# Sorted sync queue, held side streams and the gating norm on ScalarE, in a two-layer hybrid decoder trunk

## Chip, cores, metric

One Trainium2 chip, all 8 cores, one batch element per core, no exchange between cores. The metric is the device time of the slowest core in microseconds (us), lower is better. Executions come in two states: *fast*, and *slow*, in which one die (cores 0 to 3 or 4 to 7) or both run at a lower granted TensorE clock. Only fast executions are compared; where a kernel had few of them, the text says so and uses the cores of an undisturbed die (their longest span). An execution that counts as fast can still hold a short stretch at the lower clock (0.81 in the clock records); where the clock records show one that matters, the text says it.

## The reference

Two layers, each a feed-forward, a mixer and a second feed-forward, every one behind an RMSNorm with a shift, scale and gate computed from a conditioning vector; sequence 4096, width 1024, hidden width 2816.

```python
for l in range(DEPTH):
    mod = c_act @ ada_w[l] + ada_b[l]                 # "ada" columns: shift, scale, gate x 3
    y = modulate(rmsnorm(h, norm_g[l, 0]), sh1, sc1)
    h = h + 0.5 * g1 * swiglu(y, ffn1_wg[l], ffn1_wu[l], ffn1_wd[l])
    y = modulate(rmsnorm(h, norm_g[l, 1]), sh2, sc2)
    u_a, v_a, q_b, k_b, v_b = split(y @ w_in[l])
    out_a = spatial_gating(u_a, v_a, ...)             # gelu, layer norm of v, 128x128 causal matmul
    out_b = dilated_mixture(rope(q_b), rope(k_b), v_b)   # 8 heads, three window/dilation patterns
    h = h + g2 * (concat([out_a, out_b]) @ w_out[l])
    y = modulate(rmsnorm(h, norm_g[l, 2]), sh3, sc3)
    h = h + 0.5 * g3 * swiglu(y, ffn2_wg[l], ffn2_wu[l], ffn2_wd[l])
return rmsnorm(h, final_g)
```

## The kernel before

Everything is unrolled at build time. `Sched` collects five instruction lists, one per engine, in *program order*, and adds semaphore waits from the buffers that an operation reads and writes. The TensorE's list is therefore a static order. The main stream (feed-forward, projections) calls `tick(ns)` after each piece, and `Mix` spends that credit on *side streams*: norms of the next tiles, attention, the conversion of float32 weights to bf16 copies in DRAM, the ada columns. h (`hS`), the normed input (`y2S`), q, k, v (`qS`, `kS`, `vS`) and the mixer's output (`mS`) travel through DRAM.

```python
def dma(self, eng, key, fn, reads=(), writes=(), accw=(), extra=()):
    ...
    self._waits(eng, self._deps(reads, writes, accw, extra))   # eng "sp": one queue, program order
    ...
class Mix:
    def tick(self, ns):
        for s in list(self.sides):
            s[1] += ns
            while s[1] > 0 and s in self.sides:
                ...
                s[1] -= next(s[0])          # emit one unit of the side stream, pay its cost

def conv_gen(l, w, cost): ...               # wguS/wdS <- wgu/wd, DRAM to DRAM, issued by POOL
def norm_load(t, src, bsrc):                # one 2 MB load
    Sx.dma("sp", "h", lambda e: e.dma_start(out=hbuf[0], in_=src[t]), ...)
def norm_steps(cost, mode, l, i, t, src, bsrc, y=0, gate=None, load=True, head=3):
    norm_load(t, src, bsrc)
    for _ in range(head):
        yield cost
    for q in range(4):
        norm_sq(2 * q); norm_sq(2 * q + 1)          # ScalarE squares (L535)
        if q: norm_mm(2 * q - 2); norm_mm(2 * q - 1)  # TensorE sums (L540)
        yield cost
    ...

def load_res(q):                            # feed-forward: residual tile of h for the down projection
    Sx.dma("sp", "hres%d" % (q % 3), lambda e: e.dma_start(out=ap, in_=src[tiles[s], :, m, :]), ...)
def down(q):                                # 22 matmuls (L668), then h + gate * result on VectorE (L675)
    ...
    Sx.dma("sp", "hres%d" % (q % 3), lambda e: e.dma_start(out=hS[t, :, m, :], in_=ap), ...)
    ...
def mixer_prep(l, t0, out):                 # 20 loads of w_in (512 KB float32 each) at once, issued by POOL
    for c in (1, 2, 0, 3, 4):
        for q in range(4):
            Sx.dma("pool", "win%d" % c, lambda e, n=n: e.dma_start(out=mx.win[0][:, n], in_=win_d[l, n]), ...)
        ...
def vnorm(s):                               # layer norm of the gating values, VectorE (L840)
    for hd in range(4):
        Sx.op("dve", lambda e, k_=k_, hd=hd: e.tensor_scalar(
            out=vh[:, hd, :], in0=vg[:, hd, :], scalar1=mv[:, k_, 0:1], scalar2=rs[:, k_:k_ + 1],
            op0=ALU.subtract, op1=ALU.mult), ...)
def load_qk(p):                             # attention, head pair p
    for h in range(2):
        srck = bass.AP(kS.tensor, kS.offset + row, [[128 * S, 2], [S, 32], [1, n]])
        ...                                 # and the same for q: four loads
def outproj(l, tiles, ox, banks, loaded, flag):
    ...
    for i, (t, m) in enumerate(pairs):
        ...                                 # 8 matmuls (L1158)
        ...                                 # h + gate * result on VectorE (L1163)
        Sx.dma("sp", "oh%d" % (i % 6), ... out=hS[t, :, m, :], in_=ap ...)
        load_h(i + 4)                       # residual tile of h, six buffers
```

The softmax here doesn't subtract the row's maximum and nothing guards it: scores larger than these inputs give would overflow.

Of the kernel before, what the change touches and what calls it, by code (L numbers as in the profile page):

```python
# [6 lines left out]
F32 = mybir.dt.float32  # L7
# [49 lines left out]
class Sched:  # L57
    ENG = ["pe", "act", "dve", "pool", "sp"]

    def __init__(self, nc, stack):  # L60
# [8 lines left out]
        self.sym = {e: [] for e in self.ENG}  # L69

# [44 lines left out]
    def op(self, eng, fn, reads=(), writes=(), accw=(), sig=True, extra=()):  # L115
        self._waits(eng, self._deps(reads, writes, accw, extra))
        if sig:
            self.cnt[eng] += 1
            s = self.sem[eng]
            self.q[eng].append(lambda e, fn=fn, s=s: fn(e).then_inc(s, 1))  # L120
            self.sym[eng].append(("i", ("e", eng), 1))
            tok = ("e", eng, self.cnt[eng])
        else:
            self.q[eng].append(fn)
            tok = ("e", eng, self.cnt[eng] + 1)
# [3 lines left out]
    def dma(self, eng, key, fn, reads=(), writes=(), accw=(), extra=()):  # L129
# [3 lines left out]
        self._waits(eng, self._deps(reads, writes, accw, extra))  # L133
        self.dcnt[key] += 16
        s = self.dsem[key]
        self.q[eng].append(lambda e, fn=fn, s=s: fn(e).then_inc(s, 16))
        self.sym[eng].append(("i", ("d", key), 16))
        tok = ("d", key, self.dcnt[key])
        self._mark(tok, reads, writes, accw)
        return tok  # L140

# [57 lines left out]
def build_nc():  # L199
# [37 lines left out]
    with ExitStack() as st:  # L237
# [62 lines left out]
        class Mix:  # L300
# [9 lines left out]
            def tick(self, ns):  # L310
                for s in list(self.sides):
                    s[1] += ns
                    while s[1] > 0 and s in self.sides:
# [5 lines left out]
            def until(self, s, cond):  # L319
                while not cond():  # L320
                    next(s[0])

            def drain(self, s):
                if s in self.sides:
                    for _ in s[0]:
                        pass
                    self.sides.remove(s)
# [73 lines left out]
        def ada_mm(ap, b, col):  # L401
            for kc in range(KC):
                Sx.op("pe", lambda e, kc=kc: e.matmul(ps[:, 7, col:col + 1], lhsT=ap[:, kc, :], rhs=cact[:, kc:kc + 1],
                                                      start=(kc == 0), stop=(kc == KC - 1)),
                      reads=[b, bConst], accw=[psB[7]], sig=(kc == KC - 1))
# [18 lines left out]
        def ada_gen(lo, cols, cost):  # L424
# [3 lines left out]
            def load(i):  # L428
                ap, b = ring[i % n]
                Sx.dma("pool", "adar%d" % (i % n), lambda e: e.dma_start(out=ap, in_=ada_w[cols[i]]), writes=[b])  # L430
# [3 lines left out]
            for i, col in enumerate(cols):  # L434
                if i + n - 1 < len(cols):
                    load(i + n - 1)
                ap, b = ring[i % n]
                ada_mm(ap, b, col)
# [8 lines left out]
        class Weights:  # L447
# [6 lines left out]
            def load_gu(self):  # L454
# [10 lines left out]
                if g == 0:  # L465
                    Sx.dma("pool", "gud%d" % s, lambda e: e.dma_start(out=ap, in_=wgu_d[l, w, j]), writes=[b])
# [5 lines left out]
            def load_wd(self):  # L472
# [10 lines left out]
                if g == 0:  # L483
                    Sx.dma("pool", "wdd%d" % s, lambda e: e.dma_start(out=ap, in_=wd_d[l, w, m]), writes=[b])
                else:
                    assert bWD[l, w, m].w, ("not converted", l, w, m)
                    Sx.dma("sp", "wd%d" % s, lambda e: e.dma_start(out=ap, in_=wdS[l, w, m]),
                           reads=[bWD[l, w, m]], writes=[b])
# [24 lines left out]
        def conv_gen(l, w, cost):  # L513
            toks = [None] * 4
            i = 0
            for j in range(FC):
                toks[i % 4] = Sx.dma("pool", "cv%d" % (i % 4), lambda e, j=j: e.dma_start(out=wguS[l, w, j], in_=wgu_d[l, w, j]),
                                     writes=[bWG[l, w, j]], extra=[toks[i % 4]])
                i += 1
                yield cost  # L520
            for m in range(KC):
                toks[i % 4] = Sx.dma("pool", "cv%d" % (i % 4), lambda e, m=m: e.dma_start(out=wdS[l, w, m], in_=wd_d[l, w, m]),
                                     writes=[bWD[l, w, m]], extra=[toks[i % 4]])
# [6 lines left out]
        def norm_load(t, src, bsrc):  # L530
            Sx.dma("sp", "h", lambda e: e.dma_start(out=hbuf[0], in_=src[t]), reads=bsrc[t], writes=hbuf[1])

        def norm_sq(kc):
            ap, b = sqr[kc % 4]
            Sx.op("act", lambda e: e.activation(out=ap, in_=hbuf[0][:, kc, :], func=AF.Square),  # L535
                  reads=[hbuf[1][kc]], writes=[b])
# [38 lines left out]
        def norm_steps(cost, mode, l, i, t, src, bsrc, y=0, gate=None, load=True, head=3):  # L575

            if load:
                norm_load(t, src, bsrc)
                for _ in range(head):
                    yield cost  # L580
            for q in range(4):
                norm_sq(2 * q)
# [9 lines left out]
            while gate is not None and not gate():  # L592
                yield cost
# [24 lines left out]
        def ffn_group(l, which, tiles, src, bsrc, posts=(), nxt=(), lag=0, hook=None):  # L618
# [35 lines left out]
            def load_res(q):  # L654
                if q < len(dn):
# [3 lines left out]
                           reads=[bsrc[tiles[s]][m]], writes=[b])  # L659

            def down(q):
# [5 lines left out]
                for j in range(FC):  # L667
# [4 lines left out]
                    if j in (7, 14):  # L672
# [6 lines left out]
                       reads=[b], writes=[bHS[t][m]])  # L679
                tick(7.4 * MM)  # L680

            sp_ = mix.add(seq(*[norm_steps(4000.0, *p) for p in posts])) if posts else None
            sn_ = None
            for j in range(FC + lag):
                for s in range(2):
                    jj = j - (lag if s else 0)
                    if 0 <= jj < FC:
                        gate(s, jj)
                        if s == 1:
                            if g == 0:  # L690
                                W.keep_gu(jj)
# [735 lines left out]
```

## Time and profile before

| | before |
|---|---|
| time, median | 6319.25 us over four executions (6304.29 to 6319.44 fast, one slow at 6548.12) |
| TensorE idle in the profiled execution | 1220.7 us of 6311.8 |
| TensorE busy at half clock | 442 us, so 221 us lost |
| TensorE waits for q/k loads | 306.7 us |
| TensorE waits for sums of squares | 335.0 us |

A waits line has the waiting engine and line, what ended the wait, and then us in total, number of waits, longest. First the TensorE's small waits for the two residual sums (L675 in the feed-forward, L1163 in the output projection):

```profile
PE ps L1158 <- DVE arena L1163: 20.4, 4, 6.6
...
PE ps L668 <- DVE arena L675: 3.9, 1, 3.9
```

Then what VectorE waits for in the same two lines:

```profile
DVE arena L675 <- DMA arena<-hS: 399.8, 52, 45.8
...
DVE arena L1163 <- DMA arena<-hS: 137.7, 45, 36.3
```

VectorE often waits for residual tiles, yet hardly anyone waits for VectorE: several PSUM banks lie between.

### The profile page before, as it was taken

Reading aid. Unit: us, or ns where it says so; the run is one execution under the profiler, and the core shown is the slowest. Engines: PE = TensorE matmul, PEld = TensorE weight load, DVE = VectorE, ACT = ScalarE, POOL = GpSimd, SP = SyncE. Lnnn points to the kernel's source line nnn. Section 1 sums busy time; section 2 is a strip of 40 time slices with the busy share of each in tenths; the row PEclk is TensorE's granted clock in tenths of the full one; section 3 lists DMA queues with packets and bytes.
Section 4 is the critical chain, followed back from the end, with each engine's and each line's share of the span. In section 5 each row is a group of like instructions: output and inputs, shape, how many; then the busy total and the mean of one; then the engine's idle time right before and its main releaser. Section 6 shows DMA issues by size and latency. Waiting matters only on the chain.

```text
span 6311.8 us, 82365 instructions; the slowest of 8 cores (6270.0 to 6311.8 us)
## 1 busy us (share of the span) xinstructions
PE 5091.1 (81%) x27299; PEld 2363.6 (37%) x27826; DVE 2475.9 (39%) x4066; ACT 1838.4 (29%) x2653; POOL 588.9 (9%) x631
## 2 busy tenths in 40 slices
PE   6887768887858787689997997888868677787997
PEld 2333324443323333334443443444323333343443
DVE  2232554342634333133332337544437333433442
ACT  2220323451313333122121214344322233422321
POOL 1001220001310000100001002100022000010000
PEclk9988889998879898789998998999989888988998
DMA  8878553535464553676478554344263634336444
GB/s 178 198 181 180 160 118 97 172 103 136 132 172 127 134 136 90 146 210 172 132 182 155 177 166 136 106 129 141 96 160 116 192 92 149 130 116 216 161 156 127
DMA packets 433581, 927.65 MB, mean 147 GB/s; under 512 B 157168, under 2 KB 206704, under 8 KB 419056
## 3 DMA queue, kind: packets, MB, share of 16 engines
q1 hardware_dynamic: 388912, 785.62, 39.1%
q0 software_dynamic: 44256, 136.73, 14.3%
q8 instruction: 234, 3.83, 0.3%
q14 instruction: 179, 1.47, 0.1%
HBM read 861.26 MB, written 249.56 MB: 176 GB/s over the span
## 4 chain that ended last, share of the span: by engine, by line
PE 55%; DMA 27%; DVE 4%; ACT 4%; issue 4%; POOL 3%; SPq 2%; another core or an unknown queue 1%; DVEq 0%; ACTq 0%; POOLq 0%
PE ps L637 32%; PE ps L668 11%; DMA arena<-hS 8%; DMA arena<-qS 8%; PE ps L806 5%; DMA hS<-arena 3%; DMA arena<-xP 3%; PE ps L1058 2%; POOL arena L1092 2%; PE ps L1029 2%; PE ps L540 2%; DMA vS<-arena 2%; DMA arena<-ada_w 1%; PE ps L1158 1%; DMA mS<-arena 1%
## 5 line engine op out<-in xcount | busy, mean ns | idle before, releaser
L637 PE MATMUL ps<-arena 128*128 128x512 bf16 x10961 | 2588.7, 387 | 100.5 <-DVE arena L645 35.3
L637 PEld LDWEIGHTS ps<-arena 128*128 128x128 bf16 x11264 | 1080.8, 99 | 1348.3 <-issue 177.8
L668 PE MATMUL ps<-arena 128*128 128x512 bf16 x5489 | 1296.5, 390 | 174.2 <-DMA arena<-wdS 154.2
L645 DVE SCALAR_TENSOR_TENSOR arena<-arena,ps 128x512 f32<-128x512 f32 x704 | 483.0, 686 | 1329.0 <-ACT arena L642 1307.7
L668 PEld LDWEIGHTS ps<-arena 128*128 128x128 bf16 x5632 | 548.6, 100 | 827.8 <-issue 239.6
L642 ACT ACTIVATE arena<-ps 128x512 f32<-128x512 f32 x704 | 419.3, 596 | 1355.4 <-PE ps L637 1170.6
L647 DVE TENSOR_TENSOR arena<-ps,arena 128x512 bf16<-128x512 f32 x704 | 486.9, 692 | 442.8 <-PE ps L637 405.3
L675 DVE SCALAR_TENSOR_TENSOR arena<-ps,arena 128x512 f32<-128x512 f32 x256 | 192.1, 750 | 1139.5 <-PE ps L668 431.8
L806 PE MATMUL ps<-arena 128*128 128x512 bf16 x2522 | 606.4, 397 | 6.2 <-DVE arena L675 1.9
L1036 ACT ACTIVATE arena<-ps 128x1024 bf16<-128x1024 f32 (+1 forms) x384 | 358.1, 933 | 721.8 <-PE ps L1029 716.6
L535 ACT ACTIVATE arena<-arena 128x512 bf16<-128x512 f32 x448 | 251.9, 621 | 781.7 <-DMA arena<-hS 693.5
L1029 PE MATMUL ps<-arena 64*128 64x128 bf16 x2752 | 160.2, 233 | 368.7 <-DMA arena<-qS 306.7
L540 PE MATMUL ps<-arena 128*128 128x512 bf16 x429 | 148.4, 419 | 337.8 <-ACT arena L535 335.0
L1092 POOL TENSOR_TENSOR arena<-arena 64x512 bf16<-64x512 f32 x128 | 161.4, 1261 | 2629.4 <-ACT arena L1086 2540.6
L806 PEld LDWEIGHTS ps<-arena 128*128 128x128 bf16 x2560 | 257.0, 101 | 317.4 <-issue 50.2
L569 ACT ACTIVATE arena<-arena 128x512 bf16<-128x512 f32 x384 | 263.6, 721 | 328.7 <-DVE arena L560 243.5
L1043 DVE TENSOR_TENSOR arena<-arena 128x1024 bf16<-128x1024 bf16 (+1 forms) x384 | 242.3, 631 | 213.7 <-ACT arena L1036 209.6
L1029 PEld LDWEIGHTS ps<-arena 64*128 64x128 bf16 x2752 | 99.2, 119 | 531.5 <-issue 531.1
L1158 PE MATMUL ps<-arena 128*128 128x512 bf16 x1000 | 248.9, 408 | 47.8 <-ACT arena L888 25.6
L873 POOL TENSOR_TENSOR arena<-arena 128x512 bf16<-128x512 f32 x128 | 235.4, 1942 | 536.8 <-DVE arena L840 424.0
L560 DVE SCALAR_TENSOR_TENSOR arena<-arena 128x512 f32<-128x512 f32 x384 | 277.8, 769 | 11.1 <-ACT arena L547 10.9
L1058 PE MATMUL ps<-arena 128*128 128x128 bf16 x2736 | 222.8, 224 | 35.7 <-ACT arena L1067 18.7
(61 smaller groups left out, 2133.8 us busy)
## 6 DMA issues: line engine op xcount, KB each, us to landing
arena<-wguS SPq DMA_DIRECT2D x330, 512.0 KB, 4.1
hS<-arena SPq DMA_DIRECT2D x384, 256.0 KB, 3.9
arena<-hS SPq DMA_DIRECT2D x48, 2048.0 KB, 10.1
arena<-wdS SPq DMA_DIRECT2D x120, 704.0 KB, 5.7
arena<-hS SPq DMA_DIRECT2D x320, 256.0 KB, 5.4
wguS<-wgu POOLq DMA_DIRECT2D x66, 512.0 KB, 14.0
arena<-ada_w POOLq DMA_DIRECT2D x120, 256.0 KB, 6.0
arena<-vS SPq DMA_DIRECT2D x32, 768.0 KB, 9.1
```

Source lines behind the costliest of these rows:

```text
L560: Sx.op("dve", lambda e: e.scalar_tensor_tensor(out=hk, in0=hk, scalar=Av[:, b0:b0 + 1], in1=rstd[0], op0=ALU.mult, op1=ALU.mult), reads=[ ...
L637: Sx.op("pe", lambda e, kc=kc, half=half, bk=bk: e.matmul(bank(bk), lhsT=gu[:, half, kc, :], rhs=y[:, kc, :], start=(kc == 0), stop=(kc == ...
L642: Sx.op("act", lambda e: e.activation(out=sg, in_=bank(G), func=AF.Tanh, scale=0.5), reads=[psB[G]], writes=[bsg])
L645: Sx.op("dve", lambda e: e.scalar_tensor_tensor(out=sg, in0=sg, scalar=1.0, in1=bank(G), op0=ALU.add, op1=ALU.mult), reads=[psB[G]], write ...
L647: Sx.op("dve", lambda e: e.tensor_tensor(out=fx.act[s][0][:, j, :], in0=bank(U), in1=sg, op=ALU.mult), reads=[psB[U], bsg], writes=[fx.act ...
L668: Sx.op("pe", lambda e, j=j: e.matmul(bank(bk), lhsT=wd[:, j, :], rhs=act[:, j, :], start=(j == 0), stop=(j == FC - 1)), reads=[bwd, ba[j] ...
L806: Sx.op("pe", lambda e, kc=kc, lhs=lhs, rhs=rhs: e.matmul(bank(bk), lhsT=lhs, rhs=rhs, start=(kc == 0), stop=(kc == KC - 1)), reads=[bw[c ...
L1029: Sx.op("pe", lambda e, qa=qa, ka=ka, h=h, c=c: e.matmul(ps[:, QB + h, c:c + 128], lhsT=ka, rhs=qa, start=True, stop=True), reads=[bq, bkb ...
L1036: Sx.op("act", lambda e: e.activation(out=pv, in_=ps[:, QB:QB + 2, c0:512], func=AF.Exp, scale=0.125), reads=[psB[QB], psB[QB + 1]], write ...
L1058: Sx.op("pe", lambda e, v=v, vi=vi, h=h, b=b, pc=pc, o=o, prev=prev: e.matmul(o, lhsT=v[:, vi, h * 64:h * 64 + 128], rhs=pT[:, h, pc, b, : ...
L1092: Sx.op("pool", lambda e, d=d, hs=hs, h=h, as_=as_: e.tensor_tensor(out=ob[hs, :], in0=acc[hs, h, as_], in1=rc[hs, d * T:(d + 1) * T], op= ...
L1158: Sx.op("pe", lambda e, kc=kc, m=m, bk=bk, mxt=mxt: e.matmul(bank(bk), lhsT=ox.w[0][:, m, kc, :], rhs=mxt[:, kc, :], start=(kc == 0), stop ...
```

## The change

The intent is to give the TensorE no reason to stand. The scheduler now carries an estimate of each engine's time and of each transfer's landing. (1) Transfers of the sync queue are collected and issued in order of estimated readiness. (2) Units of side streams are emitted only when the estimate says that their inputs are there. (3) The gating layer norm moves from VectorE to ScalarE. Not in the short description: q and k are stored so that a head pair is one 128-partition block, with one load each in place of two; the norm's load is cut in four; bf16 weight copies and the conversion are moved and spaced.

```diff
+    def when(self, deps): ...                       # estimated time at which deps are fulfilled
+    def ok(self, *bufs):
+        return self.force or all(self.when(b.w) <= self.t["pe"] for b in bufs)
     def dma(self, eng, key, fn, ...):
-        self._waits(eng, self._deps(reads, writes, accw, extra))
+        ready = self.when(deps)
+        if eng == "sp":
+            ready = max(ready, self.lastd.get(key, 0.0))
+            self.spq.append((ready, len(self.spq), deps, fn, key))
+        self.dfree = max(self.dfree, ready) + ns
+        self.est.setdefault(("d", key), []).append(self.dfree + 3500.0)
+    def order_sp(self):
+        for _, _, deps, fn, key in sorted(self.spq, key=lambda x: x[:2]):
+            self._waits("sp", deps)
     ... (cut)
             for q in range(4):
+                while not Sx.ok(*hbuf[1][2 * q:2 * q + 2]):
+                    yield 500.0
                 norm_sq(2 * q)
     ... (cut: the same hold for ada columns, q/k units and P.V units)
-                    Sx.op("dve", lambda e: e.tensor_scalar(out=vh[:, hd, :], in0=vg[:, hd, :], ...
+                    Sx.op("act", lambda e: e.activation(out=vh[:, hd, :], in_=vg[:, hd, :],
+                        func=AF.Identity, scale=rs[:, k_:k_ + 1], bias=nm[:, k_:k_ + 1]), ...
     ... (cut)
-                for h in range(2):        # k and q, [[128 * S, 2], [S, 32], [1, n]] each
+                Sx.dma("sp", "ak", lambda e: e.dma_start(out=k[:, k0:2 * SB], in_=kS[p, :, 0:n]), ...)
+                Sx.dma("sp", "aq", lambda e: e.dma_start(out=q, in_=qS[p, :, T0:T0 + SB]), ...)
     ... (cut: stores of q and k, quarter loads of h, spacing of the conversion, cap of 12 us on credit)
```

## The prediction

110 + 30 + 10 + 20 + 30 + 130 + 90 + 90 = 510 us of idling leave 711 of the 1220.7 saved, with 130 of cold clock 6319 - 711 - 130 = 5478, and with 60 for the rivals 5540. L840 is the gating norm on VectorE; "On it there already" speaks of ScalarE in a projection tile of 35.5 us, and the 12 us of slack are the seven banks that the kernel uses, each with 8 matmuls at the 0.22 us that are measured there (39 in 8.58 us).

A long gap is one over 3.4 us; the shortest clock record is 3.41 us. In the profiled core of the kernel before, 89 of the 92 such gaps that lie between matmuls have a record at half clock that overlaps their end or begins at most 3.41 us after it (one more long gap stands before the first matmul). Of the seven slices with busy digit 9 in the first fence, six have clock digit 9 and one has 8.

> **What bounds the kernel now.** I read the page's head first, then the waits of the TensorE, then single stretches and single transfers.
>
> ```profile
> span 6311.8 us, 82365 instructions; the slowest of 8 cores (6270.0 to 6311.8 us)
> PE 5091.1 (81%) x27299; PEld 2363.6 (37%) x27826; DVE 2475.9 (39%) x4066; ACT 1838.4 (29%) x2653; POOL 588.9 (9%) x631
> ...
> PE   6887768887858787689997997888868677787997
> ...
> PEclk9988889998879898789998998999989888988998
> ```
>
> No other engine comes near the TensorE. It idles 6311.8 - 5091.1 = 1220.7 us. Where its busy digit is 9 the clock digit is 9; where the busy digit falls, the clock falls too. The stretch table shows the same on two neighbours:
>
> ```profile
> 3002.00:3160.00 158.00, 157.00 (x851) 73.61 (x867) 59.09 (x87) 30.61 (x51) 10.02 (x19) 1.00 0.49 128
> ...
> 3318.00:3476.00 158.00, 114.44 (x561) 52.18 (x571) 42.27 (x63) 28.44 (x45) 21.07 (x41) 0.86 0.91 157
> ```
>
> The first has 157.00 us of matmuls in 158 at full clock, so the machine can run this work without gaps; the second lost 43.6 us. The waits view of the TensorE says for whom it idles:
>
> ```profile
> PE ps L540 <- ACT arena L535: 335.0, 29, 42.9
> PE ps L1029 <- DMA arena<-qS: 306.7, 16, 31.6
> PE ps L668 <- DMA arena<-wdS: 154.2, 12, 27.2
> PE ps L902 <- DVE arena L840: 92.6, 20, 8.7
> PE ps L1029 <- ACT arena L1036: 62.0, 16, 8.0
> PE ps L403 <- DMA arena<-ada_w: 47.4, 8, 14.5
> PE ps L637 <- DVE arena L645: 35.3, 2, 33.3
> ```
>
> Few long waits (us in total, times, longest) make nearly all of it: the norm's sums of squares (29 waits), the attention's q/k loads (16), the down weights (12). None is in the feed-forward itself; side streams, placed statically in the TensorE's order, arrive before their data. Behind the first line is one more step: the squares' line L535 itself waits 693.5 us for loads of hS. Counting the timeline, 93 gaps are over 3.4 us.
>
> [...] its clock records hold only 1.0 and 0.5, and after an 8.20 us gap at 366 us 8 matmuls took 3.44 us (430 ns each), then 39 took 8.58 (220). Laid over the busy time, the records put 442 us of it at half clock: 221 us lost, 2.4 us per long gap. [...] The q and k loads have source dimensions [2, 32, n][...]:
>
> ```profile
> 1053.59 24.56 DMA arena<-qS
> ...
> 1917.54 39.51 DMA arena<-qS
> ```
>
> The first group moves 1 MB (q and k, two halves each, 4 x 256 KB), 43 GB/s; the second 1.5 MB. The issues table has a 1024 KB load with 128 partitions in front at 8.1 us:
>
> ```profile
> arena<-y2S SPq DMA_DIRECT2D x16, 1024.0 KB, 8.1
> ```
>
> [...]
>
> ```profile
> L840 DVE TENSOR_SCALAR arena<-arena x256: 327/343/4679, 685.1 to 4860.3; 128x128 bf16<-128x128 f32 x128
> ```
>
> Its median is 343 ns, its longest 4679, its mean in the groups 989: in the timeline a long one stands beside rope tiles on POOL (L873, mean 1942). [...]
>
> **The change, part by part.**
>
> *Queue order.* The sync queue now issues by estimated readiness instead of program order. This takes away head-of-line blocking: in the queue's own waits, 1754.3 us stand before a transfer that waits for L637 and 405.7 for L1092, with ready transfers behind. The clearest victims are the stores of the value tiles: L888 waited up to 37.3 us for one, and the TensorE then 33.3, 25.6 and 10.7 us (three waits, 71.6 us with small ones). I leave 10.
>
> *Held side streams.* Norm squares, ada columns, q/k and P·V units are emitted only when the estimate says their input has landed; the wait fills with feed-forward matmuls. The 2 MB norm load becomes four of 512 KB. Norms, 335.0 us: four long ones at the start (22.3, 12.1) and the end (11.7, 20.1) are forced, 66 down to 50; the eight in the output projections sum to 109 and leave perhaps 7 per projection, 28; the pair at 3433 and 3493 us (42.9, 14.8), beside a burst of weight conversion that is now spaced 27 instead of 20 us, leaves 10; the rest 22. Sum 110. Ada 47.4: the first 11 and a forced end stay, 30.
>
> *q/k layout, not in the title.* The loads become one transfer each with 128 partitions in front[...]: an estimated 8 to 10 us in place of 25 to 39. That alone is more than the gaps (13 to 32 us) need; with the hold, 306.7 leaves 20. [...]
>
> *Gating norm on ScalarE.* 256 operations leave VectorE, 207.5 us[...]. [...] On it there already: 12 gelu and value tiles at 0.59, a norm of 8 x 0.62 + 8 x 0.72 + 1.3, four table loads at 1.28, together 25 us. 16 small operations (negated mean times rstd) come on VectorE. L902's 92.6 leaves 30.
>
> *Not touched or worse.* The softmax normalisation on ScalarE (L1082 to L1086, 4.5 us a time ahead of the next exp) stays: L1029 and L637 behind L1036, 80.2, and L1058's 35.6, together 115.8, leave 100. The attention costs 4 x 52 x 1.85 = 385 us of main-stream credit, plus about 25 for its first load and 4 x 9 of holding, 446 with pauses, against some 403 between its start and its forced end; before it was 425. About 10 units run bare, at twice the TensorE's work: 30 us more over four. The down-weight waits (160.7 with wd) fall together with the preparations: at 1516 us POOL issues 20 w_in loads (10 MB of float32) at once, and the weights issued at 1519.7 land at 1542. Order helps, bandwidth stays: 90. Moving the bf16 copies from the first to the second group shifts load between stretches with DMA shares of 0.74 to 0.90. The remaining 91 us of small waits stay.
>
> The sum of idling: 110 + 30 + 10 + 20 + 30 + 130 + 90 + 90 = 510, so 711 saved. Cold clock: some 38 long gaps x 2.4 = 91 instead of 221, 130 saved. 6319 - 711 - 130 = 5478.
>
> **The rivals.**
>
> *The estimates are wrong on the chip.* The cost model gives all POOL operations 1300 ns (L873 took 1942) and its matmuls never run cold; its transfers stand in one line. Then a transfer sorted early blocks the queue as before, and a held stream is emitted too soon or so late that the forced end runs it bare. For it: the queue is still in order. Against it: weights have six buffers, and errors of some us are smaller than the 13 to 43 us they must hide. It would halve the gain of queue and holding, leaving about 5850.
>
> *Another engine becomes the bound.* [...] the new VectorE operation waits for ScalarE's Ln and Exp before the rope products. Seven PSUM banks are 12 us of slack. At worst each of 16 tiles keeps its 5 us: 80 us more, about 5560.
>
> *Transfers set the pace.* The first four slices have DMA shares of 0.74 to 0.90; if waits only turn into later weights there, 100 to 150 us come back: 5600.
>
> [...] The 474 us from 2844 to 3318 ran at 1.00 with 99% busy[...].
>
> **Range and chances.** The 5478 counts each wait as mostly hidden; for the first and second rival I add 60: 5540. If only 40% of the idling goes, it is 6319 - 488 - 90 = 5740; with 70% and a warm clock 5300. To be within 2%, over 700 of the 840 us would have to fail, although the q/k layout alone should bring some 250. Chances 0.95, 0.04, 0.01.
>
> **What would show it.** Right: waits for qS under 30 us, q/k transfers under 12 us, L840's line gone from VectorE[...], waits for L535 near 110, long gaps under 50, mean clock over 0.95. Wrong: waits for wdS at or above 150, exp waits (L1036) well over 130 from bare attention, a new TensorE wait on hS or wguS from a badly sorted queue, or ScalarE over 90% busy in projection tiles.

## The result

The changed kernel computes the right result. Its fast executions took 5974.4 and 5988.66 us, and two of the four timed ones were slow (6427.33 and 6453.42), so that the median of all four, 6207.99 us, says little. A ratio here is the record's own, made from fast runs of both kernels in the same rounds, so not quite the ratio of the times that are quoted: 0.9473, with a 95% interval of 0.9432 to 0.9514. The change gains 5.3%, some 335 us. Predicted were 5540 us and a range of 5300 to 5820: the direction was right, the gain was less than half of what was promised, and the time is outside the range. Repeated later on one chip, the changed kernel gave 5990.24, 5992.23 and 6013.72 (0.9474), so the size stands.

The line numbers have moved. The gate matmul is now L690 (was L637), the down matmul L721 (L668), its residual sum L728 (L675), the sum of squares L593 (L540), the exp L1085 (L1036), the output projection L1213 (L1158), its residual sum L1218 (L1163), the gating norm L897 (L840), the gating matmul L958 (L902).

The head of the page of the changed kernel, to be laid beside the first fence of the prediction:

```profile
span 5972.8 us, 83260 instructions; the slowest of 8 cores (5933.9 to 5972.8 us)
PE 5060.5 (85%) x27295; PEld 2343.2 (39%) x27826; DVE 2325.6 (39%) x3826; ACT 1928.9 (32%) x2909; POOL 604.8 (10%) x661
...
PE   6987768889667889789999988798878698998997
...
PEclk9998889999888999899999999899989899999998
```

The TensorE idles 5972.8 - 5060.5 = 912.3 us, 308 us less than before; predicted were 711 less. Its time at half clock fell from 442 to 353 us, so the loss from 221 to 176 us; predicted was 91. These two differences are the whole miss: 5478 us, the sum before the allowance for the rivals, + (912 - 510) + (176 - 91) = 5965, against 5973 in this execution. So nothing but idle time, and the clock that goes with it (2.4 us lost per long gap in both kernels: 221 over 93, 176 over 73), has to be explained.

The waits of the TensorE in the changed kernel, which answer to the seven lines of before:

```profile
PE ps L1213 <- DVE arena L1218: 131.6, 48, 23.3
PE ps L690 <- DVE arena L698: 108.0, 17, 28.1
PE ps L721 <- DVE arena L728: 99.7, 9, 32.8
PE ps L1078 <- ACT arena L1085: 97.6, 18, 11.7
PE ps L593 <- ACT arena L588: 86.5, 27, 17.3
PE ps L958 <- ACT arena L897: 56.7, 7, 17.1
...
PE ps L690 <- DVE arena L728: 33.0, 9, 10.3
PE ps L860 <- DVE arena L728: 28.9, 3, 12.5
...
PE ps L1078 <- DMA arena<-qS: 2.3, 1, 2.3
```

The q/k loads are gone from the list (306.7 to 2.3) and the sums of squares fell from 335.0 to 86.5. But the top of the list is new: the two residual sums, which before had cost 20.4 us and 14.0, now cost 131.6 and 99.7 + 33.0 + 28.9 = 161.6. They are VectorE lines, and VectorE was not slower. What it waits for:

```profile
DVE arena L728 <- DMA arena<-hS: 466.0, 80, 49.9
...
DVE arena L1218 <- DMA arena<-hS: 281.8, 99, 27.8
```

In the output projection the wait for residual tiles doubled (137.7 to 281.8 us), and in the feed-forward it grew too (399.8 to 466.0). This time the slack in PSUM did not suffice. These totals alone do not convict the sort: with the queue unsorted (below) they are still 239.5 and 414.3 us. What differs is how much of them reaches the TensorE. The prediction had listed "a new TensorE wait on hS" as a sign of a badly sorted queue; it is here, one engine removed, since the TensorE waits for VectorE and VectorE for the tile.

Two predicted signs did come. The q loads, in the view of their tile, time from issue to landing (smallest, median, largest):

```profile
DMA to landing us min/median/max: 4.5/7.1/9.9
```

The groups of q and k loads in the fence of before, 1 and 1.5 MB, took 24.56 and 39.51 us. And the gating norm's line is gone from VectorE; its heir on ScalarE (smallest, median, largest in ns):

```profile
L897 ACT ACTIVATE arena<-arena x256: 477/481/494, 672.7 to 4636.7; 128x128 bf16<-128x128 f32 x128
```

481 ns is the median here; on VectorE, in the kernel before, it was 343, with a mean of 989. The rope tile on POOL did not change with the norm gone from VectorE: it has a mean of 1924 ns (1942 before). Two signs failed: the long gaps are 73, not under 50; and the mean clock is 0.932, not over 0.95.

### Three places in the trace

*The sort at work.* The sync queue, in time order, at the first output projection of the second layer (start us, us, engine, line, out<-in, count). L1203 loads a residual tile, L1221 stores one, L1020 and L1028 load the values for the first head pair of the attention that runs *after* this projection (its matmuls begin at 4781.7 us):

```profile
4652.09 0.42 SPq L1203 DMA_DIRECT2D arena<-hS  x1
...
4662.73 0.37 SPq L1020 DMA_DIRECT2D arena<-vS  x1
4663.25 9.82 SPq L1028 DMA_DIRECT2D arena<-vS  x7
4673.22 4.07 SPq L1221 DMA_DIRECT2D hS<-arena  x4
4681.28 0.32 SPq L1203 DMA_DIRECT2D arena<-hS  x1
```

and the TensorE in the same stretch:

```profile
4688.24 3.57 PE L1213 MATMUL ps<-arena 128*128 128x512 bf16 x8 [22.99 <-DVE arena L1218]
```

The value loads could go, since their inputs were there, so the sort put them first. The next residual tile left 29 us after the last one, and the TensorE stood for 22.99 us. The value tiles were not yet wanted.

*The burst.* The preparation of a mixer stage lets POOL issue twenty loads of w_in, 10 MB, at once. POOL, VectorE and TensorE around it:

```profile
1484.15 10.67 POOL L815 DMA_DIRECT2D arena<-w_in  x20
```

```profile
1517.50 0.75 DVE L728 SCALAR_TENSOR_TENSOR arena<-ps,arena 128x512 f32<-128x512 f32 x1 [40.86 <-DMA arena<-xP]
```

```profile
1518.40 11.23 PE L721 MATMUL ps<-arena 128*128 128x512 bf16 x43 [23.76 <-DVE arena L728]
```

The sync queue issued the residual tiles at 1497.2 and 1498.6 us and they came at 1517.5, some 20 us later, where the median load of such a tile takes 6.8. Once issued, the transfer no longer waits for its place in the queue. From 1497 to 1517.5 us the DMA share is 1.02, of which 0.46 is POOL's queue and 0.56 the sync queue: the DMA engines were full. The w_in loads are not all of it: in the run without them (no_burst, below) the same tile came 12.6 us after its issue and the TensorE stood for 11.81 us here. Before the tile stand, in the same queue, loads of y2S of 1024 KB each for the next stage.

*The inherited wait.* The chain in order of time at 757 us, where a store of y2 (L622 makes the tile) stands before the gating norm (start us, us, what):

```profile
757.75 6.59 DMA y2S<-arena
...
765.39 1.64 ACT arena L897 x4
...
767.16 0.27 PE ps L958
```

The norm needs nothing of y2. It stands behind L622 in ScalarE's list, and L622 waits for a buffer whose store is late. On VectorE it had not had this neighbour.

### The profile page after: what moved, and what is told of

It is laid out like the page before. It is cut to its first block, busy times and chain, and to the rows that moved or that the text cites. A ratio compares the mean times of both kernels' runs of the same rounds, so it can differ in the third digit from the quotient of the medians.

```text
span 5972.8 us, 83260 instructions; the slowest of 8 cores (5933.9 to 5972.8 us)
## 1 busy us (share of the span) xinstructions
PE 5060.5 (85%) x27295; PEld 2343.2 (39%) x27826; DVE 2325.6 (39%) x3826; ACT 1928.9 (32%) x2909; POOL 604.8 (10%) x661
## 4 chain that ended last, share of the span: by engine, by line
PE 60%; DMA 23%; ACT 5%; issue 4%; DVE 3%; POOL 3%; SPq 2%; DVEq 0%; ACTq 0%; POOLq 0%
PE ps L690 37%; PE ps L721 12%; DMA arena<-hS 7%; PE ps L860 5%; DMA hS<-arena 4%; DMA y2S<-arena 3%; PE ps L1107 2%; DMA arena<-xP 2%; DMA mS<-arena 2%; POOL arena L1141 2%; PE ps L1078 2%; DMA vS<-arena 2%; PE ps L593 1%; DMA arena<-ada_w 1%; DVE arena L613 1%
## 5 line engine op out<-in xcount | busy, mean ns | idle before, releaser
L690 PE MATMUL ps<-arena 128*128 128x512 bf16 x10954 | 2594.6, 386 | 209.2 <-DVE arena L698 108.0
L690 PEld LDWEIGHTS ps<-arena 128*128 128x128 bf16 x11264 | 1074.6, 99 | 1452.8 <-issue 291.1
L721 PE MATMUL ps<-arena 128*128 128x512 bf16 x5493 | 1279.4, 386 | 127.0 <-DVE arena L728 99.7
L698 DVE SCALAR_TENSOR_TENSOR arena<-arena,ps 128x512 f32<-128x512 f32 x704 | 483.1, 686 | 1156.1 <-ACT arena L695 1146.7
L721 PEld LDWEIGHTS ps<-arena 128*128 128x128 bf16 x5632 | 544.8, 99 | 766.6 <-issue 166.0
L860 PE MATMUL ps<-arena 128*128 128x512 bf16 x2520 | 606.1, 396 | 72.2 <-DVE arena L728 28.9
L728 DVE SCALAR_TENSOR_TENSOR arena<-ps,arena 128x512 f32<-128x512 f32 x256 | 192.2, 751 | 1078.5 <-DMA arena<-hS 466.0
L1085 ACT ACTIVATE arena<-ps 128x1024 bf16<-128x1024 f32 (+1 forms) x384 | 357.6, 931 | 423.8 <-PE ps L1078 423.8
L860 PEld LDWEIGHTS ps<-arena 128*128 128x128 bf16 x2560 | 255.8, 101 | 385.5 <-issue 122.0
L622 ACT ACTIVATE arena<-arena 128x512 bf16<-128x512 f32 x384 | 261.5, 719 | 432.2 <-DVE arena L613 233.2
L1213 PE MATMUL ps<-arena 128*128 128x512 bf16 x1002 | 253.2, 406 | 137.3 <-DVE arena L1218 131.6
L613 DVE SCALAR_TENSOR_TENSOR arena<-arena 128x512 f32<-128x512 f32 x384 | 307.7, 854 | 40.2 <-ACT arena L600 40.1
L929 POOL TENSOR_TENSOR arena<-arena 128x512 bf16<-128x512 f32 x128 | 232.9, 1924 | 530.7 <-DVE arena L919 529.7
L1107 PEld LDWEIGHTS ps<-arena 128*128 128x128 bf16 x2736 | 186.6, 99 | 159.3 <-issue 72.4
L593 PE MATMUL ps<-arena 128*128 128x512 bf16 x428 | 141.4, 399 | 91.3 <-ACT arena L588 86.5
```

Source lines behind the costliest of these rows:

```text
L613: Sx.op("dve", lambda e: e.scalar_tensor_tensor(out=hk, in0=hk, scalar=Av[:, b0:b0 + 1], in1=rstd[0], op0=ALU.mult, op1=ALU.mult), reads=[ ...
L622: Sx.op("act", lambda e: e.activation(out=out, in_=hk, func=AF.Identity, bias=modv[:, s0:s0 + 1], scale=1.0), reads=[bh, bMod[l][i]], writ ...
L690: Sx.op("pe", lambda e, kc=kc, half=half, bk=bk: e.matmul(bank(bk), lhsT=gu[:, half, kc, :], rhs=y[:, kc, :], start=(kc == 0), stop=(kc == ...
L698: Sx.op("dve", lambda e: e.scalar_tensor_tensor(out=sg, in0=sg, scalar=1.0, in1=bank(G), op0=ALU.add, op1=ALU.mult), reads=[psB[G]], write ...
L721: Sx.op("pe", lambda e, j=j: e.matmul(bank(bk), lhsT=wd[:, j, :], rhs=act[:, j, :], start=(j == 0), stop=(j == FC - 1)), reads=[bwd, ba[j] ...
L860: Sx.op("pe", lambda e, kc=kc, lhs=lhs, rhs=rhs: e.matmul(bank(bk), lhsT=lhs, rhs=rhs, start=(kc == 0), stop=(kc == KC - 1)), reads=[bw[c ...
```

## Theories and experiments

Theory: the layout is most of the gain; the sort, whose key asks when a transfer *can* go and not when it is *needed*, takes back much of what the rest earns. Rivals: (a) bandwidth, the conversion's large DRAM-to-DRAM packets or the weight bursts fill the DMA engines, whatever the order; (b) the hold pushes side streams too late; (c) ScalarE is now too full. Seventeen runs were made, three of them repeats, each with a correct result unless it says otherwise. Program order below means the changed kernel with all else as it is but the sync queue unsorted.

### The layout alone, and the change without it

The edit of the first two runs is the kernel before with this alone:

```diff
-                    Sx.dma("sp", "qk%d" % n, ... out=dst[g * 2 + h_, :, t * T:(t + 1) * T] ...
+                    to_ = bass.AP(dst.tensor, dst.offset + (g * 256 + h_ * 32) * S + t * T, [[64 * S, 4], [S, 32], [1, T]])
-                for h in range(2):  # two loads each of k and q
+                Sx.dma("sp", "ak", lambda e: e.dma_start(out=k[:, k0:2 * SB], in_=kS[p, :, 0:n]), ...)
+                Sx.dma("sp", "aq", lambda e: e.dma_start(out=q, in_=qS[p, :, T0:T0 + SB]), ...)
     ... (cut: the store issued with to_, the bodies of the two old loads)
```

> The kernel before with one part of the change: the q and k scratch laid out so that a load has 128 partitions in front. Theory of the prediction: the 16 waits for qS (306.7 us in the kernel before) nearly vanish and with them some cold clock, about 250 us less, ratio to before near 0.960. Rival (the wait only changes its name: exp on ScalarE or another load takes its place): under 100 us less, ratio 0.985 or above. In both the waits for qS should be under 40 us.

All four executions were slow, so there is no ratio. The undisturbed dies ran 6011 and 6032 us. The waits for qS were gone.

> The layout alone once more, since its first four runs all had a slow die; the undisturbed dies of those took 6011 and 6032 us. If those dies tell the truth, fast runs of 6010 to 6040 us and a ratio to before of 0.950 to 0.956: the layout alone is then nearly the whole gain of the change. Rival (undisturbed dies of a slow run gain from the idle memory of the other die): fast runs above 6100 us.

The one fast execution took 6110.39 us, and undisturbed dies of slow ones 5993 and 6007. The fast one was not free of the slower clock: of the TensorE's busy time on its slowest core, 792 us stand at 0.81 in the clock records; its two cores with no such time took 6004 and 6030. The rival, that an undisturbed die gains from the idle memory of the other, can be tried on kernels with many fast runs: in program order (below) undisturbed dies of slow runs took 5862 to 5890 us, beside fast runs of 5871 to 5883. No such gain is seen. Undisturbed dies say some 6010, that is about 300 us less than before, and the waits of the sums of squares (330.4 us) and down weights (133.3) are what they had been. The third run goes the other way, the changed kernel with the old layout:

> The changed kernel with the old q and k layout. If the layout is what emptied the qS waits, they come back to at least 100 us and the time rises by 150 to 250 us over the changed kernel (ratio to before 0.971 to 0.987). If holding the attention units alone hides the loads, the time stays within 60 us of the changed kernel (ratio 0.947 to 0.957).

Fast 6281.6 to 6333.65, ratio 0.9888 (0.9762 to 1.0014), which is unclear at 2%; waits for qS are back (190.1 us in 9). It follows that the part not named in the description carries about 300 of the 335 us. Everything else together, the sort included, is worth 20 to 70 us here (6300 us against 6319 in the first round; 71 us by the ratio on this chip), which is not clear of the noise.

### The order of the sync queue

```diff
-        for _, _, deps, fn, key in sorted(self.spq, key=lambda x: x[:2]):
+        for _, _, deps, fn, key in sorted(self.spq, key=lambda x: x[1]):
```

> The changed kernel with its sync queue issued in program order again, all else kept. Theory A (a late transfer is late because of its place in the queue, and the sort helps): the waits of the TensorE on down weights return to about 150 us and the time rises by 100 to 200 us (ratio to before 0.963 to 0.979). Theory B (a late transfer is late because the 16 engines are held by the weight conversion and by the w_in bursts, whatever the order): within 60 us of the changed kernel (0.938 to 0.957).

Fast 5870.59, 5871.07 and 5871.82 us, ratio to before 0.9216 (0.898 to 0.9451, wide because the fast runs of before on that chip went from 6333 to 6409). That is about 115 us *less* than the sorted kernel. The waits of the TensorE in program order:

```profile
PE ps L593 <- ACT arena L588: 139.5, 40, 19.3
PE ps L721 <- DMA arena<-wdS: 115.9, 9, 26.5
...
PE ps L1213 <- DVE arena L1218: 59.9, 24, 12.1
```

The down weights' wait (115.9) was 1.9 in the sorted kernel, and the sums of squares (139.5) were 86.5: the sort did cure these. But without it the residual sums fell from 131.6 to 59.9 and from 161.6 to 49.7 (42.7 + 7.0), and the attention's waits behind ScalarE from 168.4 to 117.8. The waits behind L698 fell too, from 108.0 to 60.6, but those behind L944, the same class of late stores, rose from 19.3 to 57.4, so that class hardly moved (127.3 to 118.0). The sort cures two kinds of wait and makes two others, which cost more. A repeat on another chip:

> The changed kernel with the sync queue in program order once more, on the same chip, so that the other run has its comparison beside it: 5860 to 5885 in its fast runs.

Fast 5876.03 and 5883.13: it stands. Next a key that keeps a transfer from going ahead of its place in the program, but lets it be later:

```diff
-            self.spq.append((ready, len(self.spq), deps, fn, key))
+            at = self.lastd[key] = max(ready, self.t["pe"])
+            self.spq.append((at, len(self.spq), deps, fn, key))
```

> The changed kernel with one term added to the sort: no transfer is sorted ahead of the TensorE's estimated time at the point of the program where it is emitted. Theory A1 (the sort loses because bulk loads of a later stage, the next attention's k and v and the bias rows, jump ahead of residual loads that are needed at once): the output projection's waits fall from 131.6 to about 60 us and the time by 60 to 115 us (ratio 0.929 to 0.938). Theory A2 (the sort loses because the estimated times of near neighbours are wrong): within 40 us of the changed kernel (ratio 0.941 or above).

Fast 5899.38 to 5945.91, median 5906.6, ratio 0.9341 (0.927 to 0.9412): 80 to 85 of the 115 us are back, and the output projection's residual wait fell to 91.1. Moving transfers *forward* past those that are needed at once is the larger part of the loss. Then a key from compute times alone, without estimated landings, on the thought that those landings are what is wrong:

```diff
-            self.spq.append((ready, len(self.spq), deps, fn, key))
+            at = max(self.t["pe"], self.when({k: n for k, n in deps.items() if k[0] == "e"}))
+            at = max([at, self.lasta.get(key, 0.0)] + [self.ats.get((k, n), 0.0) for (kind, k), n in deps.items() if kind == "d"])
+            self.lasta[key] = self.ats[(key, self.dcnt[key])] = at
+            self.spq.append((at, len(self.spq), deps, fn, key))
```

> The queue is sorted by the later of the program point and the estimated ends of compute instructions alone; the estimated ends of transfers, which the cost model puts in one line one after another, are left out. Theory A2b (the remaining loss of the sort, 5906 against 5871 us, is in these ends): at or under program order, 5820 to 5875 us, ratio 0.922 to 0.930. Rival: as not_earlier, 5890 to 5920 us.

A miss: fast 6261.79 and 6321.75, ratio 0.9966 (0.9853 to 1.0079). The sync queue itself now stood 1489.8 us, 299 times, for stores of hS to land (521.8 us, 158 times, in the sorted kernel; 285.0 in program order). That fits loads that read what has just been stored and now come directly behind the store, which no further run tested. If so, the estimated landings, rough as they are, do useful work.

### The hold

```diff
     def ok(self, *bufs):
-        if self.force:
-            return True
-        return all(self.when(b.w) <= self.t["pe"] for b in bufs)
+        return True
```

with the fixed head starts of before (three units in a norm, 16 us in attention) put back.

> The changed kernel with nothing held back: side units are emitted without asking for their inputs, with the fixed pauses of the kernel before. Theory of the prediction: the waits of the norm sums on ScalarE return from 86 to 250 us or more and the time rises by 150 to 250 us (ratio to before 0.971 to 0.987). Rival (the sorted queue and the four-part load already bring the tiles in time): under 60 us more (ratio 0.957 or below).

Fast 5933.88, 5952.69 and 6006.55, ratio 0.9361 (0.9169 to 0.9554). It was expected to be slower and is not; with the interval so wide and 0.9474 inside it, no gain of leaving the hold out can be claimed either. The sums of squares did rise, from 86.5 to 157.1 us, as they should, and the output projection's residual wait fell from 131.6 to 77.4. With the sort, less waiting in one place goes with more in another, and no net gain of the hold is shown. The same with program order:

> Program order with nothing held back. If holding is what the change gains beside the layout (5871 against some 6020 of the layout alone), 60 to 120 us more than 5871, with the norm sums' waits above 200 us. If holding gains nothing (as in the sorted kernel, where leaving it out took 5934 against 5990 us): 5820 to 5890 us.

One fast execution, 5955.29, and undisturbed dies of 5918 and 5945 us, against 5871 to 5883 for program order with the hold. The fast one is not free of the slower clock: six of its cores have 128 to 160 us of busy time at 0.81 (an estimate from this: 24 to 30 us lost), and the longer of the other two took 5931.3 us. So here the hold gains some 40 to 75 us. The line it works on, without it:

```profile
PE ps L591 <- ACT arena L586: 273.7, 40, 20.3
```

273.7 us without the hold and 139.5 with it. So rival (b) falls: the hold does what it was meant for, where the queue does not spoil it.

### The gating norm

Program order, with the norm back on VectorE (its first form, as in the excerpt above).

> Program order, with the gating norm back on VectorE. Theory of the prediction[...]: waits of the gating matmuls rise from 40 to 70 us or more, the rope tiles on POOL stay near 1.9 us, and the time rises by 30 to 60 us over the 5871 us of program order. Rival (on ScalarE it stands behind the norm's tiles, which wait for their stores, so nothing was won): within 20 us of 5871, or less.

Fast 5906.48 and 5919.32, ratio 0.9353 (0.9324 to 0.9382), on another chip. By these two times the norm on VectorE looks some 35 us slower than program order with the norm on ScalarE. The trace says otherwise. In the profiled execution the four cores of die 0 have 112 to 136 us of busy time at 0.81 in the clock records (an estimate from this: 21 to 25 us lost), and those of die 1 have none:

```profile
die 0 (median of its cores): 5883.6 us, clock 0.932
die 1 (median of its cores): 5852.1 us, clock 0.938
```

In the two profiles of program order the four dies have medians of 5842.0 to 5859.0. The longest core of the undisturbed die took 5869.9 us, and that of die 0 in the second fast execution, at a clock of 0.935 to 0.937, 5872.2: the 5871 to 5883 us of program order. So the rival of this run holds: within 20 us, and no gain of the move is shown. The wait of the gating matmul did rise to 81.2 us (16 times, longest 10.6), from 40.2 in program order, as the theory said; the sums of squares fell (139.5 to 124.5), and all idling on the slowest core is 787 us, against 772 and 782. Rival (c) isn't borne out either, since the norm on ScalarE costs nothing that shows.

The rope tile on POOL is at 1952 ns here and at 1925 in program order, so these 256 operations are not what sets its time; what does, no run shows.

### The conversion's packets

The conversion runs in DRAM-to-DRAM packets of 22528 and 32768 bytes, which took 2.3 and 3.6 us each on their engine (means of the kernel before; 2.4 and 3.4 in the changed one). If these hold up small transfers, shorter ones should help:

```diff
+        def cut(t, off, n):
+            return bass.AP(t.tensor, off, [[1024, 16], [16384, n], [1, 1024]])
-            ... e.dma_start(out=wguS[l, w, j], in_=wgu_d[l, w, j])
+            ... e.dma_start(out=cut(wguS, wguS[l, w, j].offset, 16), in_=cut(wgu_d, wgu_d[l, w, j].offset, 16))
     ... (cut: the same for wdS and wd_d, with 22)
```

> The changed kernel with the weight conversion cut so that no piece is over 1024 elements (the trace of the changed kernel shows pieces of 32768 and 22528 bytes at 3 to 4 us each on an engine). Theory B (each small packet of the sync queue waits for one such piece on its engine): the long value-store and residual waits during conversion shrink and the time falls by 50 to 90 us (ratio 0.933 to 0.939). Rival (the conversion takes bandwidth, whatever its pieces): within 30 us (ratio 0.942 or above).

One fast execution, 5988.06 us: nothing, with the sorted queue. The repeat of the changed kernel that ran beside it:

> The changed kernel itself, as a mark beside the next ones on the same chip. Both theories: ratio to before 0.943 to 0.952, waits as in its first profile.

It gave the three times quoted under the result. In program order:

> Program order on the sync queue and the conversion cut to 1024 elements. Program order alone took 5871 us. Theory B: 50 to 90 us less, 5780 to 5820 us, ratio to before 0.912 to 0.919. Rival: 5840 to 5900 us.

Fast 5837.67, 5843.12 and 5852.69, ratio 0.923 (0.9196 to 0.9265). The ratio doesn't tell it from program order; in plain times it is 30 us below it on the same chip, without overlap, in another round. It is the fastest correct version and beats both kernels. With the compute-only key:

> The same with the conversion cut to 1024 elements. With program order the cut gave 28 us; here 0 to 40 us under engine_est. If it comes out under 5843 us it beats all versions so far.

One fast execution, 6223.86: a miss as well.

### The bursts

First an attempt to pace them: each w_in load was made to depend on the TensorE's progress, and the second w_out load was spread.

> Program order, with the w_in and the second w_out loads tied to the TensorE's progress, one group after another, in place of twenty or eight at once. Theory B2 (the late down weights and residual tiles at the four stage changes are late because the burst takes half of the engines' time): waits for wdS fall from 116 to under 60 us, those behind the residual sums too, 60 to 120 us less than 5871. Rival (the bytes only come later and the projection waits for its weights): within 30 us of 5871, with new waits for w_in.

Inconclusive. The result was wrong (relative error 0.47), for a reason that was not found, and the pacing did not take hold: sixteen of twenty w_in loads still left together, at 1487.1 us in POOL's timeline. Fast 5918.29 to 5986.24; nothing is read from it. Then the bursts were taken away, with a wrong result on purpose:

```diff
             for c in (1, 2, 0, 3, 4):
-                for q in range(4):
+                if c != 1:
+                    Sx.op("pool", lambda e, c=c: e.memset(mx.win[0][:, c * 4:c * 4 + 4], 0.01), writes=[mx.win[1][c]], ...)
+                for q in range(4 if c == 1 else 0):
                     Sx.dma("pool", "win%d" % c, ...
     ... (cut: the same for all loads of w_out)
```

> The changed kernel, wrong on purpose: 16 of 20 w_in groups of tiles and all of w_out are filled by POOL with a constant in place of being loaded, so that the bursts at the stage changes shrink to a fifth or nothing. Theory B2 (the burst delays the residual loads): the TensorE's waits for the residual sum of the down projection (161.6 us over three lines) fall under 70 us and the time by 80 to 150 us. Rival (those loads are late because of their place in the queue): the waits stay above 120 us and the time within 40 us of the changed kernel.

Fast 5878.15, 5879.18 and 5905.44, ratio 0.9332 (0.928 to 0.9385): about 105 us less than the changed kernel. The feed-forward's residual waits fell from 161.6 to 92.2 (57.9 + 29.2 + 5.1), not below 70 as expected. So bursts are a second loss. To see whether it is the sort's loss in another dress, both were undone together:

> Wrong result on purpose: the changed kernel with the sync queue in program order AND with 16 of the 20 input-projection weight loads and all output-projection weight loads of each preparation replaced by a fill of their tiles. It asks whether the two losses found so far, the sort (about 115 us) and the bursts (about 106 us with the sort), are two separate ones. Theory separate: the waits on wdS (115.9 us with program order) and on loads at stage changes fall to under 40, and the time goes to 5870 - 80 to 105, that is 5765 to 5790, inside the range that was predicted. Rival, the same waits seen twice (late residual loads that the sort makes and the bursts lengthen): with program order the bursts cost under 30 us, the time stays at 5840 or above, and wdS stays above 80 us.

Fast 5787.05 and 5808.1, against 5876.03 and 5883.13 for program order on the same chip: another 82 us. The waits of the TensorE:

```profile
PE ps L593 <- ACT arena L588: 148.6, 46, 16.9
PE ps L1081 <- ACT arena L1088: 78.1, 16, 9.8
PE ps L721 <- DMA arena<-wdS: 64.9, 5, 19.8
```

The first reading holds, that they are two losses, though the down weights stay at 64.9 where under 40 was expected. With both undone the kernel comes to about 5797 us, inside the predicted range. Its weights are wrong, so it is a measurement and not a version; and since the kernel before has the same bursts, taking them away is not undoing a part of the change. It does not vindicate the prediction, which counted the bursts as staying.

## Why the prediction was wrong

The account, from fast runs or undisturbed dies, with the differences that could be measured alone:

| step | us |
|---|---|
| before | 6319 |
| q/k layout | -300 |
| hold, gating norm, quarter loads, spacing and the rest (in program order) | -145 |
| = program order | 5874 |
| sort | +115 |
| = the changed kernel | 5989 |
| without sort and bursts | 5797 |

Of the third line the hold has some 40 to 75 and the gating norm nothing that shows; the rest, some 70 to 105, was not measured piece by piece.

**The failed step is "Queue order".** The prediction took the sort for a gain ("takes away head-of-line blocking") and counted for it the value stores (71.6 to 10) and part of the down weights (160.7 to 90, "Order helps"). Measured alone, with all else as in the changed kernel, it costs 115 us. Blocking at the queue's head had been read from the queue's own waits, where 1754.3 us stand before L637; that wait is 1708.6 in the changed kernel (L690) and 1693.0 in program order, sorted or not, so it is no measure of what a sort can win. The sort moved early-ready loads ahead of residual tiles, and the TensorE's waits for residual sums went from 34.4 to 295.5 us (109.6 in program order), a class to which the prediction gave no term. It had read that none of the long waits is in the feed-forward itself, although the down weights, third on its list, are. In its first rival it did say that "a transfer sorted early blocks the queue as before", and priced that at "halve the gain of queue and holding", about 5850, which came nearest of all its figures. But this 5850 cannot be worked out from its terms (half of what it gives to norms, ada columns, value stores and down weights is some 190 us on top of 5478), and in the point it weighed no more than its share of 60 us, for two rivals together.

**Second, "Order helps, bandwidth stays: 90".** The burst was seen and priced only where it showed then, at the down weights. After the sort those cost 18.1 us, and the same burst delayed residual tiles instead. About 80 to 105 us go when bursts go, sorted or not.

**Sizes, term by term.** The columns are us of TensorE waits in the profiled execution.

| term | before | predicted | changed | program order | without sort and bursts |
|---|---|---|---|---|---|
| sums of squares | 335.0 | 110 | 86.5 | 139.5 | 148.6 |
| q loads | 306.7 | 20 | 2.3 | 0 | 0.6 |
| attention behind ScalarE | 115.8 | 130 | 168 | 118 | 117 |
| down weights | 160.7 | 90 | 18.1 | 141.0 | 71.6 |
| residual sums | 34.4 | no term | 295.5 | 109.6 | 98.3 |
| gating matmul | 92.6 | 30 | 56.7 | 40.2 | 49.8 |
| value and y2 stores (L698, L944) | 71.6 | 10 | 127.3 | 118.0 | 109 |
| ada columns | 47.4 | 30 | 45.5 | 41.4 | 43.7 |
| all idling | 1220.7 | 510 | 912.3 | 772.2 | 698.7 |

In the last row the cores profiled for before and changed lack some 2% of their matmul records, and those of the last two columns have all. Cores with all records idle 1185 us (before) and 856 us (changed, core 1 of each), so the step from changed to program order is nearer 84 us than 140.

Waits for value stores rose. The prediction took them for victims of the queue's order, but the one at 907.8 us, 28.13 long, stands behind a store that, once issued, took 34.05 us to land with the conversion under way; for that part its place in the queue is not what it waits for. In program order the class is still 118.0 us, so the sort is not what raised it; what did was not tested. Long gaps fell from 93 to 73, not to 38, hence the cold clock's 176 us in place of 91.

**What was right.** The q/k layout, though called 250 us and worth 300; the sums of squares with the hold; the load times; that ScalarE would not become the bound (32% busy); the list of signs, which named the fault. That the gating matmul waits less (92.6 to 56.7) was right, but no gain in time came of it. But the "0.95 faster" rested on the layout, while the point and the range rested on the parts around it; a range from the layout alone (6069, by its own 250 us) to everything hidden (5478) would have been the honest one, and its lower end of 5300 does not follow from its own terms: 70% of the idling and all 221 us of cold clock give 5244.

**What stays open.** Why the rope tile on POOL takes 1.9 us; why the paced kernel was wrong; the hold and the sort's interplay, which is only described; what the parts of the change that were not run alone are worth; and the last 250 us between 5797 and 5540. In the last column of the table 189 us idle (698.7 - 510; nearer 225, since the 510 was worked out from a core with missing records) and 78 us cold (169 - 91) stand over what was predicted; the largest excesses are the value and y2 stores (99 us), the residual sums (98) and the sums of squares (39), none of them taken apart by experiment.

## What to carry to other kernels

Order a queue by when a transfer is needed, not by when it can go: a load that is ready early and wanted late does harm in front of one that is wanted now. Program order, which follows the need roughly, was the best of the orders tried; readiness used only to hold a transfer back still lost some 30 us to it, and an order by estimated need was not tried. When an operation moves to another engine, list what stands before it in that engine's order, since it inherits those waits: here the move won nothing that shows. And look at how a transfer is laid out before any scheduling: here one q load of 512 KB with 128 partitions in front took 7.1 us, where four q and k loads of 256 KB in the old layout had taken 24.56 together, and that undeclared detail was worth more (about 300 us) than the scheduling.

## The slower clock in the traces

What decides whether an execution falls in the slow state is not shown. In the fast profile of the kernel before, all eight cores held 1.00 from 3002 to 3160 us with the TensorE busy for 157 to 158 of the 158; a slow execution of almost the same program, the layout alone, has 0.81 at the same 99% (us, busy of each engine with instructions, then clock, DMA share and GB/s):

```profile
3000.00:3160.00 160.00, 158.70 (x705) 68.09 (x718) 47.93 (x72) 38.13 (x59) 7.92 (x15) 0.81 0.55 150
```

Of all executions recorded, 19 of 35 of the kernel before in the later rounds and 44 of 85 of the other kernels were slow, so the denser kernels were not hit more often. The clock records of the changed kernel's profiled execution hold no 0.81; some other fast runs have it in short stretches (up to 136 us on a core in the one with the gating norm on VectorE).
